# One decoder layer on one core: 26 weight blocks split in the first feed-forward and kept in DRAM, all 16 gate projections among the attention's work

## The chip, the core and the metric

The kernel runs on one of the eight cores of a Trainium2 chip. Its engines work side by side, each through its own list of instructions in order: PE (TensorE, the matrix products), DVE (VectorE), ACT (ScalarE), POOL (GpSimd) and SP (SyncE, which issues nearly all transfers here). The metric is the time of one execution in microseconds, as the median of several. The profiles show one execution each.

## What is computed

One decoder layer for 512 tokens with 1024 channels, in float32. Cut to what matters:

```python
h = x + 0.5 * swiglu(rmsnorm(x), ffn1)
u = rmsnorm(h)
p = u @ w_in                       # 3992 columns: q, keys, values, branch gates, ga, gb
A = nsa(q, compressed, selected, window 512)      # keys and values compressed by a small GELU network
B = sliding_window(sq, sk, sv, window 128, sinks)
m = sigmoid(ga) * (A @ w_branch_a) + sigmoid(gb) * (B @ w_branch_b)
h = h + m @ w_out
h = h + 0.5 * swiglu(rmsnorm(h), ffn2)
out = rmsnorm(h)
```

With eight selection blocks and 16 to be chosen, every block is chosen, so the selected branch is a causal attention over all keys. `ga` and `gb` have 1024 columns each: 16 blocks of 128, the gate projections.

## The kernel before

**Three products for one.** A float32 product is made of three in a reduced format. Each operand is split into a high part (a cast) and a low part (the source minus the high part): `mm3` multiplies high by high, high by low and low by high. Activations are split where they arise (`uh`, `ul`, `G`). A weight block of 1024 by 128 is loaded into one of four raw buffers (`W.load`), cast by ACT into the ring `whi` (`W.high`, L93) and subtracted by DVE or POOL into `wlo` (`W.low`, L97). Both rings have four slots, so block i + 4 needs the slot of block i.

**Stages.** The first feed-forward works in thirds of its 22 column blocks: gate and up products with `swiglu`, then eight down products (`ffn`). Then comes the mixing stage, in which a planner (`Schedule`) writes one order for all engines: it takes tasks with guessed lengths, and at each step emits the one that can start first. Its tasks are projections on PE in small pieces (`filler`, of the lowest rank), the splits of their weight blocks (`prepare`), and the attention units (`attend`): scores, least score, exponentials, weighing, transposes, the product with the values. First the 8 units of the sliding window (swa), then the 8 of NSA with three parts each. A pair of weight blocks is used by one `project` (96 products of 256 columns) or by one half of a compression (`compress`, 16 products of 256 columns); the order of pairs is cmp_k, SQ, cmp_k, SLC, cmp_v, Q, cmp_v, WIN, Q + 4 behind the first three. After them nine gate projections (`gate_early`, 24 products of 512 columns, eight for `ga` and one for `gb`) are fillers; their results go to DRAM (`zd`).

**The merge.** For each of eight channel blocks d: both gates are loaded from `zd` and scaled by POOL (`load_z`), or, for the seven that were not made early, made here by 24 products; then the sigmoid (ACT), the two branch products (12 each, of 512 columns), two multiplications (DVE), the sum (POOL) and its split. Then w_out, and the second feed-forward.

The engines' lists are fixed when the kernel is built: an instruction that waits holds all that stand behind it on its engine.

Of the kernel before, what the change touches and what calls it, by code (L numbers as in the profile page):

```python
# [25 lines left out]
BIG = 1e30  # L26
GB_EARLY = 1
NEVER = 1e9
# [26 lines left out]
def f32(ap):  # L55
    return ap.bitcast(F32)


class Weights:
# [6 lines left out]
    def __init__(self, tc, ctx):  # L66
        self.nc = tc.nc
        self.raw_pool = ctx.enter_context(tc.tile_pool(name="wraw", bufs=self.RAW))
        pool = ctx.enter_context(tc.tile_pool(name="wring", bufs=1))
        self.hi = pool.tile([128, self.SLOTS, 8, 128], F32R, name="whi")  # L70
        self.lo = pool.tile([128, self.SLOTS, 8, 128], F32R, name="wlo")
        self.blocks = []
        self.raw = []
        self.apart = {}
        self.prepped = 0
        self.pos = 0

    def plan(self, ap, nk):
        self.blocks.append((ap, nk))

    def load(self, n):
        while len(self.raw) <= n and len(self.raw) < len(self.blocks):
            ap, nk = self.blocks[len(self.raw)]
            t = self.raw_pool.tile([128, 8, 128], F32, name="raw")
            self.nc.sync.dma_start(t[:, :nk], ap)
            self.raw.append(t)
# [141 lines left out]
def layer(ctx, tc, a, out):  # L228
# [39 lines left out]

    def plan_in(c0, n):
        for c in range(c0, c0 + n, 128):  # L270
            W.plan(cols(a["w_in"], WIN, 0, KD, c, 128), KD)

    def plan_compress(n, r):
        for c in range(2):
            W.plan(cols(a[n], 256, r * 1024, 8, c * 128, 128), 8)

# [8 lines left out]
    plan_in(C_SLC, 256)  # L285
    plan_compress("cmp_v_w1", 0)
    plan_in(C_Q, 256)
    plan_compress("cmp_v_w1", 1)
    plan_in(C_WIN, 256)
    plan_in(C_Q + 256, 256)  # L290
    plan_in(C_GA, D)
    plan_in(C_GB, GB_EARLY * 128)
    for d in range(KD):
# [177 lines left out]

    def ffn(after, begun=(), side=None, finish=None, sums=None):

# [11 lines left out]
        for third, (f0, f1) in enumerate(THIRDS):  # L485
            for f in range(f0 + (len(begun) if f0 == 0 else 0), f1):
# [23 lines left out]

    with pool("h1") as h_pool, pool("temp1", 2) as temp, pool("start") as start:
        h = h_pool.tile([128, KD, S], F32, name="h")
        x = start.tile([128, 4, D], F32, name="x")
        rows = start.tile([128, 128], F32, name="rows")
        posi = start.tile([128, 128], I32, name="posi")
        w_in0 = start.tile([128, KD, 2, 256], F32, name="w_in0")
# [45 lines left out]

        sums0 = start.tile([128, 4], F32, name="sums0")
        x_sq = start.tile([128, D], F32, name="x_sq")
# [26 lines left out]
        def side_work():  # L591
# [11 lines left out]
            yield  # L603
            yield from rope_tables(start)

# [3 lines left out]

        ffn(to_mix, begun, side_work(), sums=sums0)  # L610


    with ExitStack() as mixing:
# [61 lines left out]
        r_turn, r_ql, r_pt, r_up = Ring(2), Ring(1), Ring(2), Ring(1)  # L675
        r_p, r_pw, r_pc = Ring(3), Ring(2), Ring(2)
        PREP, FILL = -2, 9000
        engine = {"dve": vector, "pool": gpsimd}
        fill = [None]
        used, prepped = {}, {}  # L680

# [11 lines left out]
        def prepare(first, n):  # L693

            for half in range(2):
                for i in range(first, first + n):
                    if i < W.prepped:
                        prepped[i, half] = None
                        continue
                    nk = W.blocks[i][1] // 2  # L700
                    k = slice(half * nk, half * nk + nk)
                    us = nk * 128 / 960 + 0.07
                    t = task(("act", us), lambda i=i, k=k: W.high(i, k.start, k.stop), (used.get(i - W.SLOTS),),
                             rank=PREP)

                    def low(e, i=i, k=k, half=half):
                        W.low(i, k.start, k.stop, engine[e])
                        if half:
                            W.load(i + W.RAW)
# [336 lines left out]
        def gate_early(d):  # L1046
# [266 lines left out]
        with pool("merge", 2, side="right") as mp:  # L1313
# [9 lines left out]
            for d in range(KD):  # L1323
# [117 lines left out]
```

## Time and profile before

| | |
|---|---|
| median of three runs | 1145.99 us (1145.62 to 1146.36) |
| the profiled execution | 1143.02 us |
| its span, first to last instruction | 1141.3 us |
| PE busy | 1117.3 us, 98% |
| DVE busy | 652.8 us, 57% |
| ACT busy | 440.9 us, 39% |
| POOL busy | 132.1 us, 12% |

Busy time is a sum over stages. Matrix products are pipelined: a product of 512 columns shows some 390 ns, and the next starts 227 ns after it. So a rate is read from the starts of many, and a busy PE is not yet one at its full pace. The first feed-forward lasts to about 374 us of the span, the mixing stage's planned part from there to 640, the merge and w_out to about 770.

### The profile page before, as it was taken

Reading aid. Unit: us, or ns where it says so; the run is one execution under the profiler, and the core shown is the slowest. Engines: PE = TensorE matmul, PEld = TensorE weight load, DVE = VectorE, ACT = ScalarE, POOL = GpSimd, SP = SyncE. Lnnn points to the kernel's source line nnn. Section 1 sums busy time; section 2 is a strip of 40 time slices with the busy share of each in tenths; the row PEclk is TensorE's granted clock in tenths of the full one; section 3 lists DMA queues with packets and bytes.
Section 4 is the critical chain, followed back from the end, with each engine's and each line's share of the span. In section 5 each row is a group of like instructions: output and inputs, shape, how many; then the busy total and the mean of one; then the engine's idle time right before and its main releaser. Section 6 shows DMA issues by size and latency. Waiting matters only on the chain.

```text
span 1141.3 us, 14617 instructions
## 1 busy us (share of the span) xinstructions
PE 1117.3 (98%) x5583; PEld 939.8 (82%) x5583; DVE 652.8 (57%) x1227; ACT 440.9 (39%) x858; POOL 132.1 (12%) x137
## 2 busy tenths in 40 slices
PE   8999999999999999999999899999999999999997
PEld 6888888888888999888888688888888888888875
DVE  4564345643547599999889644565443344433453
ACT  4432122321323356757777533333222133222432
POOL 0100000000005221422112222240000000000001
PEclk9999999999999999999999999999999999999999
DMA  7233333233225442333111345423333332333221
GB/s 226 76 111 111 92 93 111 78 107 111 74 84 155 131 111 76 83 103 84 47 38 37 101 134 157 139 88 116 97 110 94 92 101 84 111 93 92 75 73 74
DMA packets 198287, 113.34 MB, mean 99 GB/s; under 512 B 4996, under 2 KB 191944, under 8 KB 198216
## 3 DMA queue, kind: packets, MB, share of 16 engines
q1 hardware_dynamic: 197416, 111.33, 34.0%
q8 instruction: 44, 0.72, 0.3%
q10 hardware_dynamic: 800, 1.07, 0.3%
q14 instruction: 27, 0.22, 0.1%
HBM read 105.83 MB, written 6.55 MB: 98 GB/s over the span
## 4 chain that ended last, share of the span: by engine, by line
PE 88%; DVE 8%; issue 1%; ACT 1%; DMA 0%; SPq 0%; POOLq 0%; DVEq 0%; ACTq 0%
PE acc L250 32%; PE s L250 28%; PE o L250 25%; DVE wlo L97 2%; PE tp L1244 2%; DVE s L1150 1%; DVE pts L1259 1%; PE tp L250 0%; DVE osum L1287 0%; DVE pbuf L1181 0%; PE tp L870 0%; DVE h L504 0%; DVE pbuf L1179 0%; DMA w_in<-in_ffn_up_dram 0%; PE tp L1365 0%
## 5 line engine op out<-in xcount | busy, mean ns | idle before, releaser
L97 DVE TENSOR_TENSOR wlo<-raw,whi 128x1024 fp32r<-128x1024 f32 (+3 forms) x221 | 242.6, 1127 | 28.3 <-ACT whi L93 27.3
L93 ACT CAST whi<-raw 128x1024 fp32r<-128x1024 f32 (+3 forms) x223 | 189.8, 890 | 131.2 <-PE acc L250 53.8
L250 PE MATMUL acc<-uh,whi 128*128 128x512 f32 x296 | 117.1, 396 | 0.0
L250 PE MATMUL acc<-ul,whi 128*128 128x512 f32 x296 | 115.7, 391 | 0.0
L250 PE MATMUL acc<-uh,wlo 128*128 128x512 f32 x296 | 115.7, 391 | 0.0
L250 PE MATMUL s<-uh,whi 128*128 128x512 f32 x280 | 109.4, 391 | 0.0
L250 PE MATMUL s<-ul,whi 128*128 128x512 f32 x280 | 109.2, 390 | 0.0
L250 PE MATMUL s<-uh,wlo 128*128 128x512 f32 x280 | 109.0, 389 | 0.0
L250 PE MATMUL o<-uh,whi 128*128 128x512 f32 x256 | 101.2, 395 | 0.6 <-ACT uh L553 0.6
L250 PE MATMUL o<-ul,whi 128*128 128x512 f32 x256 | 100.1, 391 | 0.0
L250 PE MATMUL o<-uh,wlo 128*128 128x512 f32 x256 | 99.8, 390 | 0.0
L253 ACT CAST G<-g 128x512 fp32r<-128x512 f32 x44 | 27.3, 621 | 186.2 <-DVE g L469 186.2
L250 PE MATMUL acc<-G,whi 128*128 128x512 f32 x280 | 87.6, 394 | 0.0
L250 PE MATMUL s<-G,whi 128*128 128x512 f32 x228 | 70.3, 389 | 0.0
L250 PE MATMUL o<-G,whi 128*128 128x512 f32 x228 | 70.2, 389 | 0.0
L250 PE MATMUL acc<-whi,uh 128*128 128x256 f32 x224 | 64.7, 289 | 2.0 <-DVE v L829 2.0
L250 PEld LDWEIGHTS acc<-uh,wlo 128*128 128x128 f32 x296 | 55.6, 188 | 12.3 <-DVE wlo L97 0.4
L250 PE MATMUL acc<-wlo,uh 128*128 128x256 f32 x224 | 63.6, 284 | 1.6 <-DVE wlo L97 1.6
L465 ACT ACTIVATE s<-z 128x512 f32<-128x512 f32 x44 | 27.9, 633 | 95.7 <-DVE z L463 95.7
L250 PEld LDWEIGHTS acc<-uh,whi 128*128 128x128 f32 x296 | 55.7, 188 | 10.8 <-issue 0.2
L250 PEld LDWEIGHTS acc<-ul,whi 128*128 128x128 f32 x296 | 55.8, 188 | 10.6
L250 PE MATMUL acc<-whi,ul 128*128 128x256 f32 x224 | 63.3, 283 | 0.0
(298 smaller groups left out, 2115.3 us busy)
## 6 DMA issues: line engine op xcount, KB each, us to landing
raw<-in_ffn_gate_dram SPq DMA_DIRECT2D x42, 512.0 KB, 3.9
raw<-in_ffn_up_dram SPq DMA_DIRECT2D x42, 512.0 KB, 5.1
raw<-in_ffn_down_dram SPq DMA_DIRECT2D x38, 512.0 KB, 4.3
raw<-in_w_in_dram SPq DMA_DIRECT2D x32, 512.0 KB, 4.7
raw<-in_w_out_dram SPq DMA_DIRECT2D x8, 512.0 KB, 4.5
raw<-in_ffn_down_dram SPq DMA_DIRECT2D x8, 384.0 KB, 4.0
zd<-turn_a SPq DMA_DIRECT2D x9, 256.0 KB, 2.1
z<-zd SPq DMA_DIRECT2D x9, 256.0 KB, 2.6
```

The source lines that it names most:

```text
L93: self.nc.scalar.copy(self.place(i)[0][:, k0:k1], self.raw[i][:, k0:k1])
L97: engine.tensor_tensor(lo, self.raw[i][:, k0:k1], f32(hi), op=OP.subtract)
L250: tensor.matmul(out, lhsT, rhs, start=start, stop=stop)
L253: scalar.copy(hi, src)
L465: scalar.activation(s, z, AF.Silu)
L1150: vector.tensor_tensor_reduce(b.view[:, j], b.view[:, j], u.mask, 1.0, u.least(hd), OP.add, OP.min, u.m[:, hd:hd + 1])
L1244: tensor.transpose(ps[:w, hd], u.p[:, hd, kb * w:kb * w + w], ident)
L1259: vector.tensor_tensor(p.lo, flat(b.ps)[:w], f32(p.hi), op=OP.subtract)
```

## The change

26 blocks of the mixing stage are marked early: both halves of cmp_v, Q, WIN and Q + 4, and all 16 gates (`GB_EARLY` is now eight). During the first feed-forward, `W.early` takes one of them per step: it loads it, and a step later casts it (ACT) and subtracts (DVE) into a staging buffer, and a step later stores both parts to DRAM. In the mixing stage `fetch` loads the two parts straight into the rings, 512 KB each, where a load of 512 KB, casts and subtractions stood. All 16 gates are fillers; the merge only loads them. Their results leave through the raw buffers, three in flight, and the merge's addition moves from POOL to DVE. Pools are rearranged so that the staging buffers lie where the input was.

```diff
-GB_EARLY = 1
+GB_EARLY = KD
...
+    def early(self, pool):
+
+        raw, out = {}, {}
+        order = sorted(self.stored)
+        for n in range(len(order) + 2):
+            if n >= 2:
+                i = order[n - 2]
+                for part in range(2):
+                    self.nc.sync.dma_start(self.stored[i][part], f32(out.pop((i, part))))
+            if n < len(order):
+                i = order[n]
+                ap, nk = self.blocks[i]
+                raw[i] = pool.tile([128, nk, 128], F32, name="eraw")
+                self.nc.sync.dma_start(raw[i], ap)
+            if 1 <= n <= len(order):
+                i = order[n - 1]
+                nk = self.blocks[i][1]
+                hi, lo = (pool.tile([128, nk, 128], F32R, name=x) for x in ("ehi", "elo"))
+                src = raw.pop(i)
+                self.nc.scalar.copy(hi, src)
+                self.nc.vector.tensor_tensor(lo, src, f32(hi), op=OP.subtract)
+                out[i, 0], out[i, 1] = hi, lo
+            yield
+
+    def fetch(self, i):
+
+        for part, w in enumerate(self.place(i)):
+            self.nc.sync.dma_start(f32(w[:, :self.blocks[i][1]]), self.stored[i][part])
 
     def load(self, n):
         while len(self.raw) <= n and len(self.raw) < len(self.blocks):
+            if len(self.raw) in self.stored:
+                self.raw.append(None)
+                continue
...
-    plan_compress("cmp_v_w1", 0)
-    plan_in(C_Q, 256)
-    plan_compress("cmp_v_w1", 1)
-    plan_in(C_WIN, 256)
-    plan_in(C_Q + 256, 256)
-    plan_in(C_GA, D)
-    plan_in(C_GB, GB_EARLY * 128)
+    plan_compress("cmp_v_w1", 0, True)
+    plan_in(C_Q, 256, True)
+    plan_compress("cmp_v_w1", 1, True)
+    plan_in(C_WIN, 256, True)
+    plan_in(C_Q + 256, 256, True)
+    plan_in(C_GA, D, True)
+    plan_in(C_GB, GB_EARLY * 128, True)
...
+                if early is not None:
+                    next(early, None)
...
+                if early is not None and d % 2:
+                    next(early, None)
...
-        ffn(to_mix, begun, side_work(), sums=sums0)
+        starting.close()
+        with pool("stage", 2) as stage:
+            ffn(to_mix, begun, side_work(), sums=sums0, early=W.early(stage))
...
-        PREP, FILL = -2, 9000
+        r_p, r_pw, r_pc, r_z = Ring(3), Ring(2), Ring(2), Ring(3)
+        PREP, FILL, FETCH = -2, 9000, 5.0
...
+                    if i in W.stored:
+                        if half == 0:
+                            prepped[i, 0] = prepped[i, 1] = task(("sp", FETCH), lambda i=i: W.fetch(i),
+                                                                 (used.get(i - W.SLOTS),), rank=PREP)
+                        continue
...
-                z = temp.tile([128, S], F32, name="turn_a")
+                z = flat(W.raw_pool.tile([128, 8, 128], F32, name="raw"))[:, :S]
                 scalar.copy(z, b.ps)
                 nc.sync.dma_start(zd[d], z)
 
-            x = task(("act", 0.5), out, (x,), take=[(r_turn, b)], give=[(r_acc, b)], rank=-1)
-            task(("sp", 2.0), lambda: None, (x,), give=[(r_turn, b)], rank=-1)
+            x = task(("act", 0.5), out, (x,), take=[(r_z, b)], give=[(r_acc, b)], rank=-1)
+            task(("sp", 0.5), lambda: None, (x,), give=[(r_z, b)], rank=-1)
...
+        W.load(W.pos + 3)
...
-                gpsimd.tensor_tensor(y, y, z, op=OP.add)
+                vector.tensor_tensor(y, y, z, op=OP.add)
```

PE, at the second compress block of the values; `fold` and `w` are the products around its GELU, `acc<-whi,uh` a projection. Before, the 16 compress products stand further up, with 48 products of the WIN pair behind them; 24 more of that pair begin at row 2155, and the second product of the GELU stands behind those:

```order
2150 L870 MATMUL tp<-ident_r,ql 128x128 x4
2151 L250 MATMUL o<-pts,vs 128x512 x2
2152 L870 MATMUL tp<-ident_r,ql 128x128 x4
2153 L250 MATMUL o<-pts,vs 128x512 x2
2154 L250 MATMUL tp<-fold,sqacc 128x64 x2
2155 L250 MATMUL acc<-whi,uh 128x256
2156 L250 MATMUL acc<-wlo,uh 128x256
2157 L250 MATMUL acc<-whi,ul 128x256
2158 L250 MATMUL acc<-whi,uh 128x256
```

With the change, ahead of the WIN pair (the last six products of Q and the first compress products stand just above):

```order
2106 L287 MATMUL acc<-whi,G 128x256
2107 L287 MATMUL acc<-wlo,G 128x256
2108 L287 MATMUL acc<-whi,G 128x256
2109 L287 MATMUL acc<-wlo,G 128x256
2110 L287 MATMUL tp<-fold,sqacc 128x64 x2
2111 L1295 MATMUL tp<-ident,pbuf 128x128 x4
2112 L921 MATMUL tp<-ident_r,ql 128x128 x8
2113 L287 MATMUL o<-pts,v 128x512 x2
2114 L287 MATMUL tp<-w_117,sqacc 32x64 x4
2115 L287 MATMUL acc<-whi,uh 128x256
2116 L287 MATMUL acc<-wlo,uh 128x256
2117 L287 MATMUL acc<-whi,ul 128x256
```

The WIN pair's products, 72 of which stood between the compress block and the second GELU product, are gone from there; 12 transposes and two products of the NSA values stand in their place, and the whole pair behind.

PE, where the last attention unit ends (`o<-pts,vc` is its last product), before; `acc<-G` is the merge:

```order
2643 L250 MATMUL acc<-ul,whi 128x512
2644 L250 MATMUL acc<-uh,wlo 128x512
2645 L1244 MATMUL tp<-ident,pbuf 128x128 x4
2646 L250 MATMUL o<-pts,v 128x512 x2
2647 L1244 MATMUL tp<-ident,pc 32x128 x4
2648 L250 MATMUL o<-pts,v 128x512 x2
2649 L250 MATMUL o<-pts,vc 128x512
2650 L250 MATMUL acc<-G,whi 128x512 x2
2651 L250 MATMUL acc<-G,wlo 128x512
2652 L250 MATMUL acc<-G,whi 128x512 x2
```

And with the change:

```order
2605 L287 MATMUL acc<-uh,whi 128x512
2606 L287 MATMUL acc<-ul,whi 128x512
2607 L287 MATMUL acc<-uh,wlo 128x512
2608 L287 MATMUL o<-pts,v 128x512 x2
2609 L287 MATMUL o<-pts,vc 128x512
2610 L287 MATMUL acc<-uh,whi 128x512
2611 L287 MATMUL acc<-ul,whi 128x512
2612 L287 MATMUL acc<-uh,wlo 128x512
```

Gate products now stand between the unit's last steps and behind them: 207 of them up to the first of the merge.

SP, around the start of the merge, before; `zd` takes a gate's result, `z` is a gate read back:

```order
103 L85 DMA raw<-in_w_branch_a_dram 128x4x128
104 L1062 DMA zd<-turn_a 128x512
105 L85 DMA raw<-in_w_in_dram 128x8x128
106 L1062 DMA zd<-turn_a 128x512 x2
107 L1318 DMA z_5841<-zd 128x512
108 L1318 DMA z_5844<-zd 128x512
109 L1324 DMA h<-hd 128x512
110 L1318 DMA z_5848<-zd 128x512
111 L85 DMA raw<-in_w_branch_b_dram 128x4x128
112 L1324 DMA h<-hd 128x512
```

And with the change, from the last fetched block on:

```order
239 L113 DMA wlo<-early_101 128x1024
240 L122 DMA raw<-in_w_branch_b_dram 128x4x128
241 L122 DMA raw<-in_w_branch_a_dram 128x4x128
242 L1113 DMA zd<-raw 128x512 x4
243 L122 DMA raw<-in_w_branch_b_dram 128x4x128
244 L122 DMA raw<-in_w_branch_a_dram 128x4x128
245 L1370 DMA z_6213<-zd 128x512
246 L1370 DMA z_6216<-zd 128x512
247 L1376 DMA h<-hd 128x512
248 L1370 DMA z_6220<-zd 128x512
249 L1370 DMA z_6223<-zd 128x512
250 L122 DMA raw<-in_w_branch_b_dram 128x4x128
```

The loads of z stand behind the stores of the last four gates and two weight loads, and there are two for each step.

## Rows read from the trace of the kernel before

**Rows 1.** The page: span, and busy time of PE.

```profile
span 1141.3 us, 14617 instructions
...
PE 1117.3 (98%) x5583; PEld 939.8 (82%) x5583; DVE 652.8 (57%) x1227; ACT 440.9 (39%) x858; POOL 132.1 (12%) x137
```

**Rows 2.** Busy time by stage: length, engines (instructions), clock, DMA share, GB/s.

```profile
core 0: us, PE busy (x) PEld busy (x) DVE busy (x) ACT busy (x) POOL busy (x), PEclk, DMA share, GB/s
20.00:360.00 340.00, 339.98 (x1507) 280.58 (x1506) 167.99 (x237) 102.29 (x133) 12.25 (x17) 1.00 0.34 97
...
400.00:510.00 110.00, 104.46 (x859) 101.25 (x857) 104.47 (x291) 73.77 (x200) 31.76 (x31) 1.00 0.37 97
...
620.00:640.00 20.00, 16.87 (x93) 12.61 (x92) 17.44 (x61) 13.28 (x50) 2.90 (x3) 1.00 0.16 54
640.00:645.00 5.00, 5.00 (x16) 4.02 (x16) 1.32 (x4) 3.93 (x6) 0.37 (x1) 0.67 0.26 86
```

**Rows 3.** Waits of PE from 380 to 645 us: total, times, longest.

```profile
PE acc L250 <- DVE v L829: 2.0, 1, 2.0
```

**Rows 4.** Timeline of PE at the attention's end: start, length, instruction, idle before.

```profile
633.44 0.40 PE L250 MATMUL acc<-uh,wlo 128*128 128x512 f32 x1
...
636.13 0.49 PE L250 MATMUL o<-pts,v 128*128 128x512 f32 x1 [0.91 <-DVE pts L1259]
...
639.95 1.22 PE L250 MATMUL acc<-G,whi 128*128 128x512 f32 x2
...
644.36 0.63 PE L250 MATMUL o<-G,whi 128*128 128x512 f32 x2
```

**Rows 5.** Lines of DVE, 380 to 640 us: busy and mean, idle before.

```profile
L97 DVE TENSOR_TENSOR wlo<-raw,whi 128x512 fp32r<-128x512 f32 x56 | 42.9, 816 | 2.7 <-ACT whi L93 2.6
```

**Rows 6.** DMA from 1083 to 1092 us, in 40 slices; the queue's packets, MB, share.

```profile
DMA  0000079498899577997779989969799985321100
...
q1 hardware_dynamic: 576, 2.10, 67.4%
```

**Rows 7.** Timeline of SP in the same stretch.

```profile
1083.17 3.73 SPq L85 DMA_DIRECT2D raw<-in_ffn_down_dram  x4
```

**Rows 8.** Timeline of DVE and POOL early in the merge.

```profile
645.93 1.40 POOL L1319 TENSOR_TENSOR z<-z,r_b 128x512 f32<-128x512 f32 x1 [5.57 <-DMA z<-zd]
...
646.68 1.20 DVE L97 TENSOR_TENSOR wlo<-raw,whi 128x512 fp32r<-128x512 f32 x1
...
651.13 0.68 DVE L97 TENSOR_TENSOR wlo<-raw,whi 128x512 fp32r<-128x512 f32 x1
```

**Rows 9.** Tile z in the merge: count, ns min/median/max, first and last start.

```profile
L1336 ACT ACTIVATE z<-z x16: 623/630/635, 643.3 to 720.2; 128x512 f32<-128x512 f32 x16
...
L1319 POOL TENSOR_TENSOR z<-z,r_b x9: 1262/1302/1397, 637.8 to 707.9; 128x512 f32<-128x512 f32 x9
L1339 DVE TENSOR_TENSOR z<-z,acc x8: 675/681/684, 646.1 to 721.5; 128x512 f32<-128x512 f32 x8
...
L253 ACT CAST mh<-z x8: 619/620/620, 649.9 to 725.5; 128x512 fp32r<-128x512 f32 x8
L254 DVE TENSOR_TENSOR ml<-z,mh x8: 692/694/694, 650.5 to 726.2; 128x512 fp32r<-128x512 f32 x8
...
DMA to landing us min/median/max: 2.6/2.6/2.6
```

**Rows 10.** The chain that ended last: start, length, piece.

```profile
389.08 9.36 PE acc L250 x78
...
508.86 1.74 PE s L250 x16
...
647.25 5.44 PE s L250 x24
```

**Rows 11.** Timeline of PE at the GELU of the compressed values.

```profile
490.59 0.55 PE L250 MATMUL tp<-fold,sqacc 128*128 128x64 f32 x4
...
494.25 0.63 PE L250 MATMUL tp<-w,sqacc 128*32 128x64 f32 x8 [0.18 <-DVE sqacc L995]
```

More of the change, by code (lines that the diff above doesn't have):

```diff
@@ L71, in __init__ @@
         self.lo = pool.tile([128, self.SLOTS, 8, 128], F32R, name="wlo")
+        self.tc = tc
         self.blocks = []
+        self.stored = {}
         self.raw = []
@@ L76, in __init__, with plan @@
         self.pos = 0
-    def plan(self, ap, nk):
+    def plan(self, ap, nk, early=False):
+        if early:
+            i = len(self.blocks)
+            self.stored[i] = self.tc.dram_tile([2, 128, nk, 128], F32, name="early%d" % i)
         self.blocks.append((ap, nk))
+    def early(self, pool):
[23 more added lines that the diff above has]
+            self.nc.sync.dma_start(f32(w[:, :self.blocks[i][1]]), self.stored[i][part])
     def load(self, n):
         while len(self.raw) <= n and len(self.raw) < len(self.blocks):
+            if len(self.raw) in self.stored:
+                self.raw.append(None)
+                continue
             ap, nk = self.blocks[len(self.raw)]
@@ L267, in plan_ffn, with plan_in, plan_compress @@
                 W.plan(cols(a[f"ffn{n}_down"], D, f0 * 128, f1 - f0, d * 128, 128), f1 - f0)
-    def plan_in(c0, n):
+    def plan_in(c0, n, early=False):
         for c in range(c0, c0 + n, 128):
-            W.plan(cols(a["w_in"], WIN, 0, KD, c, 128), KD)
-    def plan_compress(n, r):
+            W.plan(cols(a["w_in"], WIN, 0, KD, c, 128), KD, early)
+    def plan_compress(n, r, early=False):
         for c in range(2):
-            W.plan(cols(a[n], 256, r * 1024, 8, c * 128, 128), 8)
+            W.plan(cols(a[n], 256, r * 1024, 8, c * 128, 128), 8, early)
     plan_ffn(1, 2)
@@ L470, in swiglu, with ffn @@
         split(G[:, j], G[:, 8 + j], g)
-    def ffn(after, begun=(), side=None, finish=None, sums=None):
+    def ffn(after, begun=(), side=None, finish=None, sums=None, early=None):
         norm = {}
@@ L509, in layer @@
     hd = tc.dram_tile([KD, 128, S], F32, name="hd")
-    with pool("h1") as h_pool, pool("temp1", 2) as temp, pool("start") as start:
+    with pool("h1") as h_pool, pool("temp1", 2) as temp, pool("tables") as tables, ExitStack() as starting:
+        start = starting.enter_context(pool("start"))
         h = h_pool.tile([128, KD, S], F32, name="h")
         x = start.tile([128, 4, D], F32, name="x")
-        rows = start.tile([128, 128], F32, name="rows")
-        posi = start.tile([128, 128], I32, name="posi")
+        rows = tables.tile([128, 128], F32, name="rows")
+        posi = tables.tile([128, 128], I32, name="posi")
         w_in0 = start.tile([128, KD, 2, 256], F32, name="w_in0")
@@ L561, in x_in @@
             vector.tensor_copy(h[:, d], flat(ps))
-        sums0 = start.tile([128, 4], F32, name="sums0")
+        sums0 = tables.tile([128, 4], F32, name="sums0")
         x_sq = start.tile([128, D], F32, name="x_sq")
@@ L603, in side_work @@
             yield
-            yield from rope_tables(start)
+            yield from rope_tables(tables)
         def to_mix(d):
@@ L675, in layer @@
         r_turn, r_ql, r_pt, r_up = Ring(2), Ring(1), Ring(2), Ring(1)
-        r_p, r_pw, r_pc = Ring(3), Ring(2), Ring(2)
-        PREP, FILL = -2, 9000
+        r_p, r_pw, r_pc, r_z = Ring(3), Ring(2), Ring(2), Ring(3)
+        PREP, FILL, FETCH = -2, 9000, 5.0
         engine = {"dve": vector, "pool": gpsimd}
         fill = [None]
-        used, prepped = {}, {}
+        used, prepped, loaded = {}, {}, {}
         def task(engines, emit, after=(), **kw):
@@ L702, in prepare @@
                     us = nk * 128 / 960 + 0.07
-                    t = task(("act", us), lambda i=i, k=k: W.high(i, k.start, k.stop), (used.get(i - W.SLOTS),),
-                             rank=PREP)
+                    if i - 1 in W.stored or i - 2 in W.stored:
+                        loaded[i] = task(("sp", 2.0), lambda i=i: W.load(i), (used.get(i - W.SLOTS - 1),), rank=PREP)
+                    t = task(("act", us), lambda i=i, k=k: W.high(i, k.start, k.stop),
+                             (used.get(i - W.SLOTS), loaded.get(i)), rank=PREP)
                     def low(e, i=i, k=k, half=half):
                         W.low(i, k.start, k.stop, engine[e])
-                        if half:
+                        if half and i + 1 < pos[0]:
                             W.load(i + W.RAW)
```

## The prediction

> **What bounds the kernel now.** I read the page first, then busy time by stage, then PE's named waits, then the timeline where PE waits. PE is busy 98% of a span of 1141.3 us [rows 1], and from 20 to 360, in the first feed-forward, it has no gap: 339.98 of 340 us [rows 2]. So only PE's idle time can be won, 1141.3 - 1117.3 = 24 us, and what its products take beyond their pace. What the change can reach of both lies in the attention. From 400 to 510 us PE is busy 104.46 of 110 us while DVE, with 104.47, is 95% busy; from 620 to 640 PE has 16.87 of 20; and from 640 to 645 the granted clock is 0.67 [rows 2]. The longest wait that PE has by name there is on DVE, 2.0 us for the values' low part [rows 3]. From 633.4 on the last unit runs with nothing left to fill PE [rows 4].
>
> The profiled execution took 1143.02 us, 2.97 less than the median of 1145.99. I sum against it and add the 2.97 at the end.
>
> **The tail of the attention.** The last gate matmul starts at 633.44 and the merge's first at 639.95 [rows 4]. Between them the order has eight transposes and five products. With 0.227 us for 512 columns (24 matmuls in 5.44 us) and 0.12 for 256 or less (78 in 9.36 us) [rows 10] that is 2.1 us in 6.3: 4.2 lost. Then the clock, which fell in that quiet stretch to its lower level of 1.2 GHz, makes 12 matmuls take 644.36 - 639.95 = 4.4 us instead of 2.7: 1.7 lost. In the new order gate matmuls stand between those steps, in groups of six and nine, and 207 more follow the last product: 8.6 of the 16 gates, 47 us of PE work that waits for no softmax. I take 5.4 of the 5.9 us back, and 4 to 6.5 as bounds.
>
> **The attention's first half.** Ahead of the first NSA score DVE does 42 half splits before and 19 now. In the profile 56 halves took 42.9 us, or 0.77 each where they overlap as pipelined [rows 5]: 17.7 us less. Rotary work of the last two projections moves behind that score (some 14 passes over 512 columns at the 0.68 of [rows 9]: about 9 us), and eight weighings of 256 columns move from POOL to DVE (half of that each: 2.7). So 24 us of DVE go. PE's own work ahead of it falls too, from 110.5 us to 89.0 (counted in the order, at the prices above), since 1.6 projection pairs and a compress block now follow. Before, this took 508.9 - 389.1 = 119.8 us [rows 10], so 9.3 were lost, with DVE at 95% or 114 us. At the same share the 90 that are left need 94.6 us: 5.6 lost, a gain of 3.7. Bounds: a gain of 5.5 (all named stalls gone) and none.
>
> **The fetches.** A stored block comes back as two transfers of 512 KB with 4 KB rows. The nearest row is the last third's four row blocks, of that size and shape: issued from 1083.17, 2.1 MB, the last traffic in slice 38 of 40, so done at 1091.5: 8.3 us for a pair [rows 6, 7]. (Issued 0.4 us apart instead of on DVE's pace it may be 7.4.) Weights go round four slots, so a pair's transfer starts when the pair two places ahead has been used. Mostly an 11.5 us projection (96 x 0.12) lies in between; but behind a compress block, which is only 16 matmuls or 1.9 us, it does not. That happens twice. Ahead of the first Q pair the order puts 7.5 us of compress, scores and transposes: 0.4 lost, mostly covered. Ahead of WIN it puts 16 compress matmuls (1.9), four products (0.9), 12 transposes (1.2) and the small matmuls around the GELU (about 1.0): 5.0 of 8.3 us. The GELU chain alone, 494.25 - 490.59 = 3.7 us from its first matmul to its last [rows 11], would hold PE to about 7.1. So 3.3 us are lost there, 3.7 together. Bounds: 2 (the chain alone) and 12.8, if no attention work is ready in either gap (2 x (8.3 - 1.9)). The gates' fetches have three gates, 16 us, ahead of them and cost nothing while that holds.
>
> **The merge.** Seven gate projections leave it, so a step shrinks from 48 matmuls (10.9 us) to 24 (5.45), while the work around it hardly does. DVE has two half splits of 0.68 [rows 8], two products of 0.68, the addition (0.69, from POOL) and the low part (0.69): 4.1 us. POOL has two scalings of 1.30, where it had one and the addition in twice the time [rows 9]. A z buffer comes free every second step: load 2.6, two scalings 2.6, sigmoid 0.63, product, split, product, addition, 0.62 and 0.69 for the two parts of the sum [rows 9], with 0.1 for each of eight handovers, is 10.6 us against 10.9 of PE. It just fits. At the start it does not: SP issues the first two z loads behind the last gate's store and two weight loads, about 2.4 us after that gate. They land near 5, POOL is done near 7.2, sigmoid, product and split end at 9.3, and PE wants that split's block at 3 x 2.72 = 8.2. The next block is about 1 us late for the same reason, and DVE is held up by POOL: a half split beside a scaling took 1.20 us, one without it 0.68 [rows 8]. I take 3 us for the stage. Bounds 1 and 11.
>
> The Trainium skill (SBUF — State Buffer, "SBUF: two separate sides") goes further than that row: a VectorE instruction with two SBUF inputs and a GpSimd one that reads SBUF exclude each other for the whole instruction. The trace agrees: the split of 1.20 us ends some 0.55 us after POOL's scaling [rows 8]. By the rule with no overlap at all a step would be the full sum of both engines, which is the second rival; by the row's 0.5 us it stays near PE's 5.45.
>
> **What is hidden.** The first feed-forward gets 26 casts (two halves of 0.62 as in [rows 9]) and 26 subtractions (two of 0.82 [rows 5]): 32 and 43 us in 340, where ACT has 102 and DVE 168 [rows 2]. They are issued behind the SwiGLU of their step, and the next weights are two blocks ahead, so PE sees nothing. DMA gains 26 x 1.5 MB = 41 MB on an engine share of 0.34 [rows 2]; by [rows 6] (2.1 MB at a 67% share of 9 us) this adds about 0.38, so 0.72. A store waits on SP for a subtraction issued a step before, and raw loads stand behind it, with about two blocks (10.9 us) in hand. If that cover went, some 4 us.
>
> **Sum.** -5.4 - 3.7 + 3.7 + 3.0 = -2.4: 1140.6 on the profiled execution's scale, 1143.6 as a median.
>
> **The rivals.** *Cover everywhere* (0.25): the first half loses its stalls (-5.5), WIN waits for the GELU alone (+2.1), the merge pays its start only (+1.5): -7.3, 1138.7. For it speaks that DVE is relieved just where it is 95% busy; against it, that its work there must still run ahead of PE. *The merge bound by DVE and POOL* (0.15): if products and scalings never overlap, a step is 4.1 + 2.6 = 6.7 us, eight of them 10 over PE's pace, so +7 on the sum: 1150.6. It decides once the two engines' serial share passes 5.45 us; for it speaks [rows 8], against it that the products read PSUM and need not wait. *The fetches bare, slower* (0.10): both gaps cost 6.4, and the clock falls in each as it did at 640 (1.7 each). That replaces +3.7 by +16.2: 1156.1. It decides when the second pair's last transfer lands more than about 6 us behind the work in front of it; for it speaks that a gap is entered with two pairs' transfers queued, against it that swa units are ready in the first gap. *The feed-forward starved by DMA* (0.03): +4, 1147.6.
>
> **The numbers.** The sum's own case has 0.47, with 1140.5 to 1147.5 as its range. A measurement of this kernel tells 0.2% (2.3 us) from no change: faster is below 1143.7, slower above 1148.3. About half of the sum's case lies below: 0.25 + 0.21 = 0.46 faster; 0.26 and part of the last rival, 0.28 same; 0.26 slower. The range 1137 to 1151 leaves out the bare fetches, the worse half of the bound merge and the best of the covered case.
>
> **What would show it.** Right: no weight split by DVE for these blocks in the attention; the clock at 1.00 where attention ends; PE without a gap in the last 47 us of gates; one PE wait of 3 to 4 us on a transfer ahead of WIN; a first merge wait of 1 to 3 us on a split. Wrong: PE waits on eraw or raw in the feed-forward, several waits on fetched weights, a clock below 1 at the first half, or merge steps longer than 5.6 us all through.

## The result and the profile after

The change makes the kernel slower: 1160.95 us as a median of four runs (1158.28 to 1163.61) against 1145.80, ratio 1.0132 (95% interval 1.0106 to 1.0158), or 15 us. 1143.6 was predicted, with 1151 as the upper end. The profiled execution took 1163.61 us, the longest of the four, so sums of its rows come out some 2.7 us high.

The page of the change, span and busy time, to be read beside [rows 1]:

```profile
span 1161.7 us, 14746 instructions
...
PE 1126.6 (97%) x5583; PEld 943.5 (81%) x5583; DVE 655.6 (56%) x1219; ACT 444.4 (38%) x846; POOL 119.0 (10%) x126
```

PE is busy 9 us longer, though its instructions are as many as before, and idle for 35 us where it was for 24. Where, the windows by stage tell (columns as in [rows 2]):

```profile
20.00:360.00 340.00, 339.98 (x1508) 280.60 (x1507) 197.00 (x263) 127.14 (x159) 12.00 (x16) 1.00 0.70 218
440.00:520.00 80.00, 71.45 (x528) 66.02 (x526) 57.04 (x196) 40.66 (x124) 10.57 (x13) 0.94 0.38 143
520.00:640.00 120.00, 119.78 (x692) 99.51 (x691) 101.88 (x321) 83.20 (x260) 22.43 (x35) 1.00 0.30 101
640.00:680.00 40.00, 40.00 (x179) 33.11 (x178) 1.52 (x4) 6.02 (x12) 0.00 (x0) 1.00 0.55 191
680.00:700.00 20.00, 13.64 (x52) 10.38 (x51) 4.30 (x5) 4.29 (x7) 4.95 (x4) 0.80 0.56 168
700.00:760.00 60.00, 56.34 (x231) 43.14 (x230) 41.58 (x50) 24.84 (x41) 21.62 (x15) 0.98 0.63 189
```

The same view for the attention's first half, and for the 20 us in which the change loses most of it; first two lines of the kernel before, then one of the change:

```profile
440.00:520.00 80.00, 75.51 (x608) 72.19 (x608) 76.90 (x228) 55.26 (x161) 22.29 (x25) 1.00 0.33 86
460.00:480.00 20.00, 20.00 (x165) 19.56 (x164) 19.23 (x61) 13.90 (x47) 9.45 (x11) 1.00 0.33 86
```

```profile
460.00:480.00 20.00, 15.94 (x107) 14.21 (x107) 18.93 (x72) 13.76 (x44) 2.27 (x3) 0.91 0.54 205
```

**The first feed-forward** is as it was: 339.98 of 340 us, although the DMA share rose to 0.70. **The tail** is filled: from 520 to 680 PE lacks 0.2 us, at clock 1.00, where [rows 2] has 3.1 us of idle time and a clock of 0.67. **The first half** got worse, not better: DVE's load fell from 76.9 us to 57.0 of 80, and yet PE is busy 4.1 us less, and its clock is 0.94. The mean hides where DVE was relieved: from 460 to 480, around the late start of the Q pair, it is as busy as before (18.93 us of 20 against 19.23), and only from 500 to 520, behind the gaps, does it fall to 3.51 of 20 (19.07 before). **The merge** is the largest loss: 6.4 us idle at a clock of 0.80 from 680 to 700, 3.7 us idle behind it.

**The first half in detail.** PE's named waits from 456 to 510 us (total, times, longest), the two longest of eight kinds:

```profile
PE tp L287 <- DVE sqacc L1023: 1.9, 1, 1.9
PE tp L1295 <- DVE k_t L844: 1.7, 1, 1.7
```

None of the eight is for a transfer; all are for DVE or ACT. The timeline of SP has the fetches; four transfers are one pair. The Q pair is issued from 458.43 to 459.74, the next compress pair from 461.70, WIN from 490.85:

```profile
458.43 0.32 SPq L113 DMA_DIRECT2D whi<-early  x1
...
459.74 0.43 SPq L113 DMA_DIRECT2D wlo<-early  x1
461.70 0.32 SPq L113 DMA_DIRECT2D whi<-early  x1
...
490.85 0.32 SPq L113 DMA_DIRECT2D whi<-early  x1
```

and the last transfer of the Q pair landed 7.8 us after its issue, at 467.5 (the DMA line of a window that holds this transfer alone):

```profile
DMA to landing us min/median/max: 7.8/7.8/7.8
```

PE, meanwhile, is through the compress block at 461.6 and has this in front of it (timeline of PE: start, length, instruction, idle before):

```profile
461.63 0.38 PE L853 MATMUL tp<-ident,pbuf 128*128 128x128 f32 x2
462.87 1.07 PE L853 MATMUL tp<-ident,pbuf 128*128 128x128 f32 x6 [0.86 <-ACT pbuf L889]
465.65 0.66 PE L1295 MATMUL tp<-ident,pbuf 128*128 128x128 f32 x4 [1.71 <-DVE k_t L844]
```

```profile
472.23 0.41 PE L287 MATMUL acc<-whi,uh 128*128 128x256 f32 x1
```

So Q begins at 472.23, 4.7 us after its data was there and 10.6 us after the compress block. In between stand transposes, scores and products of the sliding window, and most of these steps wait for DVE or ACT first. As cover they hold about 4 us of PE work; the rest is their waits and the lower clock. At WIN it is the same: the compress block ends near 493, the pair's last transfer lands at 498.7, and the pair begins at 502.02.

**The merge's start**, in the timeline of all engines; the last gate leaves PSUM at 684.27:

```profile
684.27 0.59 ACT L1112 COPY raw<-acc 128x512 f32<-128x512 f32 x1 [4.85 <-PE acc L287]
...
686.39 0.92 SPq L1370 DMA_DIRECT2D z<-zd  x2
...
689.29 0.39 PE L287 MATMUL o<-G,wlo 128*128 128x512 f32 x1
```

```profile
691.70 4.95 POOL L1371 TENSOR_TENSOR z<-z,r_b 128x512 f32<-128x512 f32 x4 [60.98 <-DMA z<-zd]
694.22 0.63 ACT L1388 ACTIVATE z<-z 128x512 f32<-128x512 f32 x1 [8.06 <-POOL z L1371]
694.75 0.60 ACT L130 CAST whi<-raw 128x512 fp32r<-128x512 f32 x1
...
695.41 1.22 PE L287 MATMUL s<-G,whi 128*128 128x512 f32 x2 [5.73 <-ACT whi L130]
...
701.69 0.84 PE L287 MATMUL acc<-G,whi 128*128 128x512 f32 x2
```

The z loads go out 2.1 us after the gate's copy began, and land 5.3 us later, behind two weight loads; the page of before had 2.6 for a z load [rows 9]. The first sigmoid needs the second scaling and starts at 694.22. ACT's cast of the third weight block stands behind that sigmoid, though the block's load, issued at 685.30, had landed at 688.2. PE wants this block at 689.5, since two blocks lie ready; it gets it at 695.41, and then works at the lower clock: the block ends at 701.69, 12.2 us after the last one where 2.7 would do.

**A later step**, from one cast of the sum's high part to the one two steps on:

```profile
720.29 0.62 ACT L290 CAST mh<-z 128x512 fp32r<-128x512 f32 x1 [3.21 <-DVE z L1393]
...
721.66 0.81 SPq L1370 DMA_DIRECT2D z<-zd  x2
...
724.46 3.00 POOL L1371 TENSOR_TENSOR z<-z,r_b 128x512 f32<-128x512 f32 x2 [4.75 <-DMA z<-zd]
...
724.51 1.78 DVE L1393 TENSOR_TENSOR z<-z,z 128x512 f32<-128x512 f32 x1
...
727.49 0.63 ACT L1388 ACTIVATE z<-z 128x512 f32<-128x512 f32 x1 [0.53 <-POOL z L1371]
...
728.53 0.63 ACT L1388 ACTIVATE z<-z 128x512 f32<-128x512 f32 x1
...
728.67 0.73 PE L287 MATMUL acc<-G,whi 128*128 128x512 f32 x2 [0.64 <-ACT whi L130]
...
731.18 1.55 DVE L1393 TENSOR_TENSOR z<-z,z 128x512 f32<-128x512 f32 x1
...
732.77 0.62 ACT L290 CAST mh<-z 128x512 fp32r<-128x512 f32 x1 [3.10 <-DVE z L1393]
```

The freed buffer's loads go out 1.4 us after the cast, land 2.8 us later, the two scalings take 3.0, and at 727.49 the sigmoid starts at once: it had been waiting for them, and the cast that PE waits for at 728.67 stands behind it. The step's second sigmoid stands behind that cast too (728.53), and the addition at 731.18 shares its time with the next scalings. The eight casts lie 6.8 us apart on average (from 699.76 to 747.12), PE's own work in a step is 5.45.

### The profile page after: what moved, and what is told of

It reads as the page before. It is cut to its first block, busy times and chain, and to the rows that moved or that the text cites. A ratio compares the mean times of both kernels' runs of the same rounds, so it can differ in the third digit from the quotient of the medians.

```text
span 1161.7 us, 14746 instructions
## 1 busy us (share of the span) xinstructions
PE 1126.6 (97%) x5583; PEld 943.5 (81%) x5583; DVE 655.6 (56%) x1219; ACT 444.4 (38%) x846; POOL 119.0 (10%) x126
## 4 chain that ended last, share of the span: by engine, by line
PE 86%; DVE 8%; DMA 2%; ACT 1%; issue 1%; POOL 1%; SPq 0%; POOLq 0%; ACTq 0%; DVEq 0%
PE acc L287 34%; PE o L287 24%; PE s L287 24%; PE tp L1295 2%; DVE wlo L134 2%; DVE s L1201 1%; DMA z<-zd 1%; POOL z L1371 1%; DVE pts L1310 1%; ACT whi L130 1%; DMA raw<-in_w_branch_a_dram 0%; DVE pbuf L1230 0%; PE tp L287 0%; DVE z L1393 0%; DVE osum L1338 0%
## 5 line engine op out<-in xcount | busy, mean ns | idle before, releaser
L134 DVE TENSOR_TENSOR wlo<-raw,whi 128x1024 fp32r<-128x1024 f32 (+3 forms) x177 | 205.3, 1186 | 73.5 <-ACT whi L130 72.7
L130 ACT CAST whi<-raw 128x1024 fp32r<-128x1024 f32 (+3 forms) x178 | 161.3, 940 | 116.8 <-PE s L287 39.2
L287 PE MATMUL acc<-uh,whi 128*128 128x512 f32 x368 | 144.9, 394 | 0.0
L287 PE MATMUL acc<-uh,wlo 128*128 128x512 f32 x368 | 143.7, 391 | 0.0
L287 PE MATMUL acc<-ul,whi 128*128 128x512 f32 x368 | 143.7, 390 | 0.0
L287 PE MATMUL s<-uh,whi 128*128 128x512 f32 x224 | 87.6, 391 | 0.0
L287 PE MATMUL s<-uh,wlo 128*128 128x512 f32 x224 | 87.4, 390 | 0.0
L287 PE MATMUL s<-ul,whi 128*128 128x512 f32 x224 | 87.4, 390 | 0.0
L287 PEld LDWEIGHTS acc<-ul,whi 128*128 128x128 f32 x368 | 69.3, 188 | 13.5
L287 PE MATMUL acc<-G,whi 128*128 128x512 f32 x232 | 71.8, 391 | 0.6 <-ACT whi L130 0.6
L287 PEld LDWEIGHTS s<-G,whi 128*128 128x128 f32 x268 | 51.1, 192 | 18.3 <-ACT whi L130 7.8
```

The lines of the kernel that those rows point to most:

```text
L130: self.nc.scalar.copy(self.place(i)[0][:, k0:k1], self.raw[i][:, k0:k1])
L134: engine.tensor_tensor(lo, self.raw[i][:, k0:k1], f32(hi), op=OP.subtract)
L287: tensor.matmul(out, lhsT, rhs, start=start, stop=stop)
```

## The experiments

Ratios are to the kernel before, measured on the same chip, with 95% intervals; a microsecond figure made from ratios takes 1145.8 as the base.

**1. Only the gates stored.** The ten blocks of cmp_v, Q, WIN and Q + 4 go back to load and split.

```diff
-    plan_compress("cmp_v_w1", 0, True)
-    plan_in(C_Q, 256, True)
...
+    plan_compress("cmp_v_w1", 0)
+    plan_in(C_Q, 256)
...
```

> Only the 16 gate blocks are stored; cmp_v, Q, WIN and Q + 4 are loaded, cast and subtracted in the mixing stage as in the kernel before. Theory: of the 15 us that the change lost, some 9 lie at the two places of the attention's first half where Q and WIN are fetched (PE loses 17.6 us against its pace from 440 to 520 us, 8.7 in the kernel before), the rest in the merge. So some 9 us come back, 1149 to 1155 us, and the merge keeps its gap of 5.7 us in front of its second product block. Rival (all of it lies in the merge, and the first half only shifts its waits): 1158 to 1163. Rival (the fetches of the gates cost too): PE waits for whi or wlo in the gates after the attention.

1152.46 us, ratio 1.0070 (1.0049 to 1.0092): about 7 us back. The window of the first half is that of before again:

```profile
440.00:520.00 80.00, 76.04 (x612) 72.57 (x612) 75.17 (x234) 53.50 (x165) 24.61 (x29) 1.00 0.25 73
```

The merge kept its gap (5.0 us), and no gate waited for its fetch. The rival that puts all of it into the merge is out.

**2. Nine gates early, the rest in the merge.**

```diff
-GB_EARLY = KD
+GB_EARLY = 1
```

> The change with GB_EARLY back at 1: nine gates early, seven made in the merge, ten other blocks and the nine gates stored. Theory: the merge has its 48 products a step again and hides its z loads, so its 14 to 15 us come back, but no gates are left behind the attention's last product, so the 4 to 6 us of the tail are lost again: 1149 to 1155 us, with the first half's gaps as in the changed kernel. Rival (the merge's loss is the start's alone, 6 us and its clock): 1155 to 1160. Rival (first half carries all): 1160 or more.

1156.54 us, 1.0106 (1.0085 to 1.0127), above the expected 1149 to 1155. The later steps were hidden again, but the start was not: PE waited 6.3 us there for ACT's cast, though the steps behind it are 48 products long. So the start's cost belongs to the order of SP and ACT, not to the length of a step; the range of the theory that sees the start alone held. The tail, against the first theory, stayed filled (20.00 of 20 us from 620 to 640): nine gates reach the attention's end here.

**3. The z loads issued by POOL.**

```diff
-                nc.sync.dma_start(z, zd[d])
+                nc.gpsimd.dma_start(z, zd[d])
                 gpsimd.tensor_tensor(z, z, r_b, op=OP.mult)
```

> The change with the z loads issued by POOL, each in front of its scaling, in place of SP. The first z then no longer stands behind the last gate's store and two weight loads. Theory: the gap of 5.7 us at the merge's start and the lower clock behind it go (about 8.8 us from 680 to 700), the waits of later steps stay or shrink somewhat: 1150 to 1155 us. Rival (the exclusive use by DVE and POOL sets the merge): the start is still late by the scalings, and at most 3 us come back: 1157 to 1161.

1174.70 us, 1.0266 (1.0244 to 1.0289): 15 us slower than the change by the ratios, a miss of both. The start's gap did go (from 680 to 700 PE was busy 20.00 us at clock 1.00). But POOL now waits for each load before it issues the next:

```profile
697.95 0.58 POOL L1370 DMA_DIRECT2D z<-zd  x1
701.08 1.25 POOL L1371 TENSOR_TENSOR z<-z,r_b 128x512 f32<-128x512 f32 x1 [2.55 <-DMA z<-zd]
702.28 0.58 POOL L1370 DMA_DIRECT2D z<-zd  x1
```

One z takes 4.3 us, two 8.6, for each step of 5.45.

**4. The addition back on POOL.**

```diff
-                vector.tensor_tensor(y, y, z, op=OP.add)
+                gpsimd.tensor_tensor(y, y, z, op=OP.add)
```

> The change with the merge's addition back on POOL. Theory (each step is a chain from the freed z buffer through load, scalings, sigmoids, products and addition back to it): the addition takes about 1.3 instead of 0.69 us and stands behind POOL's scalings, so the time is the same or up to 5 us longer: 1160 to 1166. Rival (DVE's own load bounds the merge): 0.69 us less of DVE per step, 2 to 5 us back: 1156 to 1159.

1172.49 us, 1.0243 (1.0217 to 1.0269): 13 us slower than the change by the ratios, in the direction of the theory and more than twice its 5 us. The addition stands on POOL behind the next step's scalings, and these behind a load whose buffer is freed by the step ahead. That makes a loop of one step, not two:

```profile
700.33 0.62 ACT L290 CAST mh<-z 128x512 fp32r<-128x512 f32 x1 [3.99 <-POOL z L1393]
...
701.70 0.81 SPq L1370 DMA_DIRECT2D z<-zd  x2
...
704.52 2.56 POOL L1371 TENSOR_TENSOR z<-z,r_b 128x512 f32<-128x512 f32 x2 [4.23 <-DMA z<-zd]
...
707.04 1.28 POOL L1393 TENSOR_TENSOR z<-z,z 128x512 f32<-128x512 f32 x1
...
708.35 0.62 ACT L290 CAST mh<-z 128x512 fp32r<-128x512 f32 x1 [5.32 <-POOL z L1393]
```

1.4 to the loads' issue, 2.8 to POOL, 2.56 and 1.28 on it, 8.0 in all, and PE waits for it. So, with the rest of the change in place, moving the addition to DVE was worth 13 us, and it is no part of the loss.

**5. The scaling taken out of the merge.** DVE scales each gate while it leaves PSUM; ACT's copy there is gone too.

```diff
-                scalar.copy(z, b.ps)
+                vector.tensor_tensor(z, b.ps, r_b, op=OP.mult)
...
-                gpsimd.tensor_tensor(z, z, r_b, op=OP.mult)
```

> The change with the scaling by r_b moved: DVE scales each gate as it leaves PSUM (in place of ACT's copy), and POOL's 16 scalings in the merge are gone. Theory (a merge step's length is the loop from a freed z buffer through load, two scalings, sigmoids, products and addition, 13 us for two steps where PE needs 10.9): 2.6 to 3 us leave the loop, so the steps run at PE's pace and the start's gap of 5.7 us shrinks to some 3: 9 to 11 us back, 1149 to 1153 us. Rival (the start alone costs, the steps are bound by SP's queue of loads): 3 us back, 1156 to 1159.

1154.29 us, 1.0085 (1.0069 to 1.0100): 5.4 us back by the ratios, between the 9 to 11 of the theory and the 3 of its rival. Part of the shortfall is that the theory rested on the profiled execution, the longest of its kernel. All steps behind the start now run at PE's pace, and the start still costs:

```profile
680.00:700.00 20.00, 15.73 (x60) 12.48 (x59) 5.45 (x9) 6.04 (x10) 0.00 (x0) 0.83 0.54 172
700.00:760.00 60.00, 60.00 (x263) 49.01 (x262) 41.27 (x54) 25.57 (x41) 8.33 (x7) 1.00 0.70 206
```

**6. Q, WIN, Q + 4 stored, cmp_v split as before.**

```diff
-    plan_compress("cmp_v_w1", 0, True)
+    plan_compress("cmp_v_w1", 0)
...
-    plan_compress("cmp_v_w1", 1, True)
+    plan_compress("cmp_v_w1", 1)
```

> The change with the two halves of cmp_v loaded and split in the mixing stage as before; Q, WIN, Q + 4 and the gates stay stored. Theory (Q and WIN are late because their 2 MB start only when the pair two places ahead is used, which is 2 us before they are wanted, and share the queue with the next compress block's 2 MB): without the second transfer Q and WIN land some 2 to 3 us sooner, but still 5 us behind the compress block; half of the first half's extra 9 us comes back: 1154 to 1158 us. Rival (it is the compress blocks' own fetch that costs): all 9 come back, 1150 to 1153. Rival (the planner's order, not the transfers): no change, 1158 to 1163.

1159.48 us, 1.0129 (1.0111 to 1.0146): not told from the change by the time. The theory's 1154 to 1158 is missed, and so is the rival that puts all 9 us on the compress blocks' fetch; the range of the rival "the planner's order" holds. In the profile PE is busy 72.37 us from 440 to 520 at clock 1.00, against 71.45 at 0.94 in the change, so there is less lost, but the merge's gaps were not the same in the two executions. It is inconclusive on its own, beyond this: the fetch of cmp_v is not the main cause.

**7. Nothing stored.** The kernel before with all 16 gates early and the addition on DVE.

```diff
-GB_EARLY = 1
+GB_EARLY = KD
...
-                gpsimd.tensor_tensor(y, y, z, op=OP.add)
+                vector.tensor_tensor(y, y, z, op=OP.add)
```

> The kernel before with two edits only: all 16 gates made early, and the merge's addition on DVE. Nothing is stored or fetched. Theory (storing buys nothing, since casts and subtractions of the gates have room, and the merge loses its 14 us whether gates were stored or not): as with only the gates stored, 1149 to 1155 us, with the merge's first gap of about 5 us. Rival (the splits of 16 gates hold the attention's second half, where DVE is 85% busy): 1156 to 1162.

1149.85 us, 1.0049 (1.0034 to 1.0065). That is run 1 or a little less, without any store.

**8. The same, with the scaling as the gate leaves PSUM.** Edits of runs 5 and 7.

> The kernel before with all 16 gates made early, the addition on DVE, and each gate scaled by DVE as it leaves PSUM (no scaling by POOL in the merge). Theory: the tail's 5 us are won, the merge's steps run at PE's pace, and only its start is late, by some 3 us: 1140 to 1145 us, at or below the kernel before. Rival (16 more passes of 0.7 us on DVE in the attention cost as much as they save): 1147 to 1152.

1144.75 us, 0.9993 (0.9982 to 1.0004): as the kernel before, the tail's gain spent on the merge's start (a gap of 1.9 us, and the clock at 0.91 from 680 to 700).

**9. Another guess for a fetch**, on the kernel of run 5.

```diff
-        PREP, FILL, FETCH = -2, 9000, 5.0
+        PREP, FILL, FETCH = -2, 9000, 3.0
```

> The kernel with the scaling on DVE (1154.3 us), with one number changed: the planner's guess for the fetch of one block, 3.0 us in place of 5.0. With 5.0 the order puts all the attention work that is at hand between a compress block and the pair behind it; with 3.0 the Q pair's first 12 products stand three attention steps earlier and the WIN pair's first 12 among the transposes. Theory (PE loses its time there in the waits of attention steps that the order sets in front of the pair, not for the pair itself, whose last transfer had landed 4.7 us before PE reached Q): 4 to 8 us of the 15 between 460 and 520 come back, 1146 to 1150 us. Rival (the transfers set it): the waits move to whi and wlo, and the time stays at 1153 to 1156.

1153.06 us, 1.0078 (1.0058 to 1.0099), against 1.0085 in run 5: the theory's 4 to 8 us did not come back, and the 0.8 us between the two is within their intervals. The time is in the rival's range (the transfers set it), though PE waited only 0.7 us for a transfer by name. Q began at 466.69 in place of 472.23, WIN at 494.66 in place of 502.02, and only there does PE name a transfer:

```profile
PE tp L1295 <- DVE k_t L844: 1.7, 1, 1.7
...
PE acc L287 <- DMA wlo<-early: 0.7, 1, 0.7
```

The waits up to k_t stayed, since they come at once behind the compress block, when no pair is there whatever the guess. The order was thus a part, and the smaller one. My reading, which run 12 supports, is that most of the loss stands because for 5 to 6 us nothing is at hand that needs neither DVE nor ACT.

**10. Only the gates stored, scaled as in run 5.**

> Only the 16 gates stored, each gate scaled by DVE as it leaves PSUM. Theory: the first half is that of the kernel before, the tail is filled, the merge loses only its start (4 us and its clock): 1143 to 1147 us, the same as with nothing stored and the same scaling (1144.75). Rival (storing relieves DVE and ACT of 16 splits in the attention's second half and pays there): 1139 to 1142.

1144.88 us, 0.9998 (0.9985 to 1.0010), the same as run 8 where nothing is stored. Storing the gates gained nothing here. The two are not alike inside, though: PE's gap at the merge's start is 4.6 us in this run's profile and 1.9 in run 8's, so storing may gain in the attention what the start costs. The edit of run 11, which closes this gap, was not tried with stored gates. Against run 5 (all 26 stored) it is 10 us less: the price of storing the other ten blocks.

**11. Run 8 with the z loads issued by POOL**, which has no scaling to do in the merge any more.

> The kernel before with all 16 gates early, the addition on DVE, each gate scaled by DVE as it leaves PSUM (1144.75 us), and the z loads issued by POOL, which has nothing else to do in the merge. Theory: the first z loads no longer stand behind the last gate's store, so the merge's first gap (2.0 us) and the clock's fall behind it (2 us) go: 1140.5 to 1142 us, faster than the kernel before by 0.2% or more. Rival (the gap is held by the sigmoid's table load and the cast behind it, which wait for z anyhow; POOL's issue costs more than SP's): 1143 to 1146.

1140.85 us, 0.9963 (0.9948 to 0.9977), faster than both kernels. Here the edit of run 3 does what it was meant to:

```profile
651.17 2.39 POOL L1318 DMA_DIRECT2D z<-zd  x4 [5.08 <-issue]
```

```profile
680.00:700.00 20.00, 20.00 (x90) 16.57 (x89) 13.18 (x20) 8.79 (x17) 3.20 (x6) 1.00 0.69 207
```

The first four loads go out at 651.17, 24 us ahead of the merge's first product (675.64), and PE has no gap there.

**12. cmp_v and the gates stored, Q, WIN and Q + 4 split**, on the kernel of run 5.

```diff
-    plan_in(C_Q, 256, True)
+    plan_in(C_Q, 256)
...
-    plan_in(C_WIN, 256, True)
-    plan_in(C_Q + 256, 256, True)
+    plan_in(C_WIN, 256)
+    plan_in(C_Q + 256, 256)
```

> The kernel with the scaling on DVE (1154.3 us), with Q, WIN and Q + 4 loaded and split in the mixing stage; both halves of cmp_v and the gates stay stored. Theory (a stored pair is late only where nothing but a compress block, 16 products, lies between the freeing of its slots and its use; that is Q and WIN; cmp_v's own fetch lies behind a projection and is covered): the first half's extra 9 us come back, 1144 to 1147 us, as with only the gates stored (1144.9). Rival (the compress blocks' fetch, 2 MB through the same queue, is itself a cause): 1149 to 1155. Second rival (four split blocks fewer relieve DVE and pay): 1141 to 1143.

1147.66 us, 1.0026 (1.0015 to 1.0037): 6.8 us of run 10's 10 come back, 0.7 us above the range of the theory. Around Q PE's gaps are down to 0.4 us each, and what is left is a wait for the split of a pair (PE's waits from 440 to 520):

```profile
PE acc L287 <- DVE wlo L134: 3.0, 3, 1.6
```

with the clock at 0.96 in this stretch.

## Why the prediction was wrong

The time lies 10 us above the range's upper end. Two rivals pointed up: the bare fetches with a falling clock (1156.1), and a merge bound by DVE and POOL (1150.6). Each was priced alone. Both losses came, but neither quite by its rival's mechanism: attention work was at hand in the gaps, and in the merge products and scalings did overlap (both below). Added to the sum together the two would have given 1163.1, near the 1160.95 partly by luck.

**The tail (-5.4 predicted): right, a little over.** Runs 8 and 11 have the filled tail and nothing stored; 11 has the merge hidden as well and is 4.2 us below the kernel before (2.6 to 6.0). That lies within the bounds of 4 to 6.5, though its interval reaches below them, and it is the tail net of all else that run 11 changes.

**The first half (-3.7) and the fetches (+3.7): this failed, at the cover.** Together they were to give zero and cost 7 us (run 1 against the change) to 10 (run 10 against 5). The transfer was priced well: 8.3 us for a pair, against 9.1 at Q and 7.8 at WIN from the first issue to the last landing. The step that failed is "ahead of WIN it puts ... 5.0 of 8.3 us", and likewise "0.4 lost, mostly covered" at Q. It counted the attention's work at PE's pace, as if PE could do it in one go. Most of those products wait for a step of DVE or ACT, and without projections between them they are a chain: 10.6 us at Q, 9 at WIN. The clock, which fell in both, came on top, and was only in a rival.

The DVE term failed with it. Up to the first NSA score, the stretch that it was worked out for, the windows are, first before, then with the change:

```profile
389.10:508.86 119.76, 114.22 (x939) 111.00 (x939) 109.31 (x303) 78.07 (x210) 31.76 (x31) 1.00 0.37 98
```

```profile
389.10:488.97 99.87, 94.08 (x748) 90.15 (x747) 87.05 (x269) 60.23 (x172) 16.24 (x16) 0.98 0.29 96
```

That 24 us of DVE work go was nearly true: 22.3. But the stretch took 99.9 us and not 94.6, so against the 89.0 of PE's work 10.9 were lost, more than the 9.3 before; the gap at Q lies in it. The gain had been read from DVE's busy share, as if PE lost in proportion to it. (The share was misread as well: 95% is that of 400 to 510 us; from 389.1 on it is 109.31 of 119.76, or 91%.) From 460 to 480 DVE is as busy in both kernels, and PE is busy 20.00 us in the one and 15.94 in the other. So what PE lacked was not a freer DVE but independent products while DVE works. Taking the splits away took the early arrival of a pair away too: a block that is split on the spot lies in a raw buffer long before its slot is free (before, SP issued the Q pair's loads from 436.52, 23 us ahead of its first product at 459.49), and DVE then needs four half splits, while a fetched pair starts its 8 to 9 us only when the slot is free. Run 12 shows the same from the other side: with these pairs split again and cmp_v still fetched, 6.8 of 10 us come back.

**The merge (+3.0, bounds 1 to 11): mis-sized.** It cost some 14 us in the profile: 9.5 at the start and about 5 behind it. By runs it is 3.4 (8 against 11, with no scaling in the chain) and 5.4 to 8.2 for the scaling (change against 5, 1 against 10). Three things were off at the start. A z load was taken as 2.6 us and needed 5.3. (The sum had a slip too: two scalings of 1.30 from 5 on end at 7.6, not 7.2.) The split behind the sigmoid was set at "3 x 2.72 = 8.2", and PE wants it after two blocks, at 5.45; with this alone my own 9.3 would have given 3.9 us. And the clock, which I had charged in the rival of the fetches, was not charged here. In the later steps the loop was put at 10.6 us for two steps; it measured 12.5 in the rows shown and 13.5 on average. In the rows shown a cast and a second sigmoid of ACT stand inside it (728.53 against 727.49: 1.0 us), where the sum had one sigmoid; the addition takes 1.55 instead of 0.69 and the two scalings 3.0 instead of 2.6.

How much of this is DVE and POOL in each other's way stays partly open. That they are is shown: beside the scalings an addition took up to 1.78 us, and without any scaling by POOL (run 5) it never took more than 0.69. These are rows of tile z, min, median and max in ns, first two of the change, then one of run 5:

```profile
L1393 DVE TENSOR_TENSOR z<-z,z x8: 691/887/1783, 699.0 to 746.4; 128x512 f32<-128x512 f32 x8
...
L1391 DVE TENSOR_TENSOR z<-z,acc x6: 674/680/686, 697.1 to 745.7; 128x512 f32<-128x512 f32 x6
```

```profile
L1392 DVE TENSOR_TENSOR z<-z,z x8: 691/693/693, 696.7 to 737.1; 128x512 f32<-128x512 f32 x8
```

The Trainium skill (SBUF — State Buffer, "SBUF: two separate sides") says that of a VectorE instruction with two SBUF inputs and a GpSimd one that reads SBUF, whichever starts first holds the shared port for its whole instruction; the addition that began 0.05 us after a scaling, at 724.51, agrees.

The second rival wanted more than that rule gives, that products and scalings never overlap. That is not so: no product with its input in PSUM took more than 0.69 us, and the one at 716.68 ran beside a scaling that began at 716.69. So the rival's 6.7 us a step is near the 6.8 measured by luck. How far the stretched instructions explain the step can be estimated. Over the eight steps additions, low parts and scalings took 8.6, 6.9 and 23.2 us; where nothing stretches them (runs 5 and 4) they take 5.5, 5.5 and 20.6. That is 7.1 us, or 0.9 for one turn of the loop, which holds one step's worth of each: without it a turn would be some 12.6 us, still over PE's 10.9. Run 4 shows that a loop sets a step without any of this: there a step took 8.0 us, the sum of its loads, scalings and addition, although behind the start no instruction of DVE in the merge was stretched. The loop sets the step; the port lengthens some of its links. No run takes out the stretching alone.

**What was to be hidden was**: the feed-forward with 26 casts and subtractions, and the gates' fetches. The DMA share of 0.70 was put at 0.72; worked out again from [rows 6], the prediction's 41 MB add 0.35 and not 0.38, which gives 0.69.

The parts add up to about the whole: -4.2, +7 to 10, +3.4 and +5.4 to 8.2 give 12 to 17 us, and 15 were measured. What each run moves in the others' gaps was not taken apart further.

## What to carry to other kernels

Work that is to cover a transfer covers it only if it can run without the engines that are late there: count it by its chain through all engines, not by its length on PE. When a projection is taken out of a merge, what becomes exposed is each loop through a buffer (load, scaling, activation, product, free), so walk that loop once per buffer, with the queue that the load stands in and every instruction in front of it on the same engine. An issue placed on an idle engine cost nothing here (run 11), and the same line on an engine that then waits for the load was a chain (run 3). A mean busy share over a stage does not say where an engine is relieved: read it in the very stretch where PE waits.

## What the runs showed of the hardware that I had not expected

Fetches of 512 KB that were issued eight at a time, at Q and at WIN, landed 5.7 to 10.1 us after their issue, where the trace has the landing; those issued two at a time for the gates landed after 3.4 to 5.7. The DMA share over the 80 us around was only 0.38: a low mean share says little about a burst. PE's granted clock fell partly to its level of 1.2 GHz in places where no single wait was long: in the change it was 0.93 on average from 480 to 500 and 0.90 from 500 to 520, after waits of 1.9, 0.9 and 0.9 us with short products between, and the first products of the WIN pair started 0.21 us apart instead of 0.12. So a stretch of waits cost twice: once itself, and once in the products behind it.
